# Attention and retention products on 64 rows run over all 128 rows, with zeros on the half that is not theirs

## The chip, the core and the metric

The kernel runs on one core of one Trainium2 chip. The metric is the device time of one execution in microseconds (us); before and after are compared by the median of several runs. TensorE (PE in the rows) multiplies with an array of 128 rows by 128 columns: a product first loads its stationary operand (a load of weights, PEld), then streams the moving operand through, a column at a time. The rows of the array are the contraction; an operand that stands on 64 of the 128 partitions uses 64 of them. VectorE is DVE in the rows, ScalarE is ACT, GpSimd is POOL, and SyncE, which issues the reads of the weights, is SP.

## The reference

Two layers over 256 tokens of width 2048. Each layer has a mixer (an mLSTM group, a retention group and a multi-head latent attention group side by side) and a feed-forward block. What the change touches is the scores of the attention and the retention:

```python
# attention, 8 heads: 128 columns without position, 64 with rotary position (k_r is shared by the heads)
q = concat([q[..., :128], rope(q[..., 128:])]);  k = concat([k_nope, broadcast(k_r)])
s = einsum('bqhd,bkhd->bhqk', q, k) * 192 ** -0.5
o = softmax(s) @ v

# retention, 4 heads with queries and keys of 64 columns, values of 128, in chunks of 128 tokens
scores  = einsum('bhnld,bhnsd->bhnls', qc, kc) * decay
y_intra = einsum('bhnls,bhnse->bhnle', scores, vc)
y_inter = einsum('bhnld,bhnde->bhnle', qc, r_start) * inner     # r_start: [64, 128], the state before the chunk
y       = y_intra + y_inter                                     # forward and backward are summed
```

## The kernel before

All weights are read once, in chunks of 128 partitions by 1024 columns (512 KB), in the order in which they are used. ACT rounds a chunk to its first part `whi`, DVE subtracts to get the rest `wlo`, and PE multiplies with both. These products (tile `pm`; `f` in the feed-forward) are the main stream. Four raw chunks and four split chunks may be in flight.

Everything else of the mixer is side work, written as generators whose steps are put between products of the main stream. A step yields the time to leave before its next step, and that time is counted in main-stream products issued (function `pump`). So the order of instructions on each engine is fixed when the program is built, and does not depend on how long anything takes on the chip.

The changed places, with the lines of the profile (every product goes through the helper `mm`, line 333, so the rows name the tiles):

- `mla_head(h)`, eight heads a layer. For each of the two tiles of 128 queries the scores (tile `sc`, 256 key columns) are a sum of three products: `qT` with `kT` (plain fp32, which the profile shows as two passes), `qrT` with `krh` (one pass), and `qrT` with `krl` (one pass) on partitions 0 to 63. `qrT` holds the first part of the rotated queries on partitions 0 to 63 and the second part on 64 to 127; `krh` is the first part of the rotated key on both halves, and `krl`, the second part of the key, exists on partitions 0 to 63 alone.
- `ret_task`, once a layer. It transposes queries, keys and scaled queries (tile `rt`, three groups, each copied out by ACT to `rT`), two heads to a tile: the even head on partitions 0 to 63, the odd head on 64 to 127. It also forms the states `R` (tile `rR`), laid out the same way.
- `ret_head(h)`, four heads a layer. The scores (tile `rs`) are two products of 128 columns on the 64 partitions of the head; the output (tile `ry`) is, for each of two tiles, a product on 128 partitions (`sd` with `rv`) and one on 64 (`rT` with `rR`). All of these are plain fp32, so each is two passes in the profile.

The tile `rT` takes the buffer `big2` that held the attention's `kT` before; `rsc` takes `big3` that held the attention's `v`.

Of the kernel before, what the change touches and what calls it, by code (L numbers as in the profile page):

```python
# [10 lines left out]
F32 = mybir.dt.float32  # L11
# [24 lines left out]
# columns of the constant array  # L36
# [5 lines left out]
# columns of a layer's parameter array  # L42
# [4 lines left out]
def weight_plan():  # L47
    """Blocks of weights in the order of their use; each is cut into chunks (k rows of tiles, columns)."""
    plan = []

    def nat(key, l, mat, kts, c0, w):
        per = max(1, CH // w)
        if not plan:
            kts0, kts = kts[:2], kts[2:]
            chunks = [([k], c0, w) for k in kts0]
        else:
            chunks = []
        chunks += [(kts[i:i + per], c0, w) for i in range(0, len(kts), per)]
        plan.append((key, l, mat, chunks))

    def stat(key, l, mat, kts, tiles):
        """One chunk per group of (tile, k) pairs, tile major."""
        per = CH // P
        pairs = [(t, k) for t in tiles for k in kts]
        chunks = [pairs[i:i + per] for i in range(0, len(pairs), per)]
        plan.append((key, l, mat, chunks))

    k16 = list(range(16))
    kout = [8, 9, 10, 11, 12, 13, 14, 15, 0, 1, 2, 3, 4, 5, 6, 7]
    for l in range(DEPTH):  # L70
        nat("c_q", l, "w_in", k16, 1024, 512)
        nat("c_kv", l, "w_in", k16, 1536, 336)
        nat("r_qk", l, "w_in", k16, 1872, 512)
        for h in range(0, 8, 4):
            stat(("kn", h), l, "w_kv_up", [0, 1], [h, h + 1, h + 2, h + 3])
        for b in range(2):
            nat(("v", b), l, "w_kv_up", [0, 1], 1024 + 512 * b, 512)
        for h in range(0, 8, 2):
            stat(("qn", h), l, "w_q_up", [0, 1, 2, 3], [h, h + 1])
        nat("qr", l, "w_q_up", [0, 1, 2, 3], 1024, 512)  # L80
        stat("ml_q", l, "w_in", k16, [0, 1, 2, 3])
        stat("ml_k", l, "w_in", k16, [4, 5, 6, 7])
        nat("ml_v", l, "w_in", k16, 2384, 512)
        nat("r_v", l, "w_in", k16, 2896, 512)
        nat("ml_o", l, "w_in", k16, 3408, 512)
        nat("r_g", l, "w_in", k16, 3920, 512)
        for part, kk in (("a", kout[:8]), ("b", kout[8:])):
            for b in range(2):
                nat(("out" + part, b), l, "w_out", kk, 512 * b, 512)
        for b in range(2, 4):  # L90
            nat(("out", b), l, "w_out", kout, 512 * b, 512)

        def ff1(g, i):
            f = g * 8 + 2 * i
            if g == 0 and i == 0:
                for half in range(2):
                    for t in range(2):
                        stat(("ff1", f + t, half), l, "w_ff1", k16[8 * half:8 * half + 8], [f + t])
            else:
                stat(("ff1", f), l, "w_ff1", k16, [f, f + 1])  # L100

        def ff2(g, b):
            nat(("ff2", g, b), l, "w_ff2", [g * 8 + i for i in range(8)], 512 * b, 512)

        for i in range(4):
            ff1(0, i)
        for g in range(NGRP):
            for i in range(4):
                if g + 1 < NGRP:
                    ff1(g + 1, i)  # L110
                ff2(g, i)
    return plan
# [8 lines left out]
def in_columns():  # L121
    """The columns of w_in in the order in which the blocks read them."""
    r = np.arange
    return np.concatenate([
        r(0, 1024), r(3600, 4112), r(4112, 4432), r(2048, 2064), r(2064, 2576),
        r(1024, 1536), r(2576, 3088), r(1536, 2048), r(3088, 3600)])
# [82 lines left out]
class Stream:  # L209
    """The weights, chunk after chunk: read, then split into two parts that one pass carries exactly."""  # L210
# [39 lines left out]
def encoder_kernel(ctx: ExitStack, tc: tile.TileContext, xin, posin, w, par, const, gfin, out, dump=None):  # L250
# [25 lines left out]
    rs2 = one.tile([P, 2], F32, name="rs2")  # L276
    ident = head[:, :P]
# [10 lines left out]
    nc.sync.dma_start(out=cst, in_=const)  # L288

    # the clock of the tensor engine rises with use: products of zeros until the data is there  # L290
# [14 lines left out]
    def rsqrt(dst, src, n, scale):  # L305
        """dst = 1 / sqrt(src * scale + EPS) on [P, n] by Newton's iteration, in steps."""
        nt = sp.tile([P, 3, n], F32, name="nt", tag=f"nt{n}", bufs=2 if n == 2 else 1)
        v, y, a = nt[:, 0, :], nt[:, 1, :], nt[:, 2, :]
        iv = a.bitcast(I32)
        V.tensor_scalar(v, src, scale, EPS, op0=ALU.mult, op1=ALU.add)  # L310
        V.tensor_scalar(iv, v.bitcast(I32), 1, None, op0=ALU.arith_shift_right)
        V.tensor_scalar(y.bitcast(I32), iv, -1.0, float(0x5f3759df), op0=ALU.mult, op1=ALU.add)
        for it in range(3):
            yield 1.0
            V.tensor_tensor(a, y, y, op=ALU.mult)
            V.scalar_tensor_tensor(a, a, -0.5, v, op0=ALU.mult, op1=ALU.mult)
            V.scalar_tensor_tensor(dst if it == 2 else y, a, 1.5, y, op0=ALU.add, op1=ALU.mult)

    def split(*items):
        """hi + lo = src (* g) of each item, both in the one-pass format."""  # L320
# [18 lines left out]
    class Task:  # L339
        """Steps of side work; a step yields the time to leave before the next one."""  # L340
# [46 lines left out]
    chunk_no = [0]  # L387

    def nat_steps(chunks, ps, lh, ll, base, first, last):
        """ps[t] += (lh + ll)[k].T @ weights for both tiles of tokens."""  # L390
# [22 lines left out]
    def stat(chunks, kts, rh, rl, dst):  # L413
        """dst[tile] = weights.T @ (rh + rl) for one tile of weight columns after another."""
# [26 lines left out]
    def make_xT(b, g0, l, wait):  # L441
        """Columns 512 b .. of x, transposed and times the gain; their sums of squares."""
# [28 lines left out]
    def new_xT(b, g0, l, square, wait=0.8):  # L471
        """Starts the transposes of block b; after the last, the scale of the tokens."""
# [46 lines left out]
    def rope(dst, src, t, n):  # L519
        """Rotates n heads of 64: src [P, n * 64], dst that or [P, n, 64], of tile t of the tokens."""  # L520
# [13 lines left out]
    def hflat(tl):  # L534
        return tl.rearrange("p a b -> p (a b)")

    def layer(l):
# [39 lines left out]
        def ckv_task():  # L577
# [15 lines left out]
            krl = L["krl"] = ap.tile([P, S], F32R, name="krl", tag="krl")  # L593
# [11 lines left out]
        def qr_task():  # L605
# [7 lines left out]
            # of each head the first part on 64 partitions, the second on the other 64  # L613
# [12 lines left out]
        def mla_head(h):  # L626
            qT, kT, qrT, krh, krl, v = L["qT"], L["kT"], L["qrT"], L["krh"], L["krl"], L["v"]
# [5 lines left out]
            for t in range(2):  # L633
# [4 lines left out]
                mm(o, qrT[0:64, h, tk], krl[0:64, :], False, True)  # L638
# [27 lines left out]
        def gate_task():  # L666
# [32 lines left out]
            # lf <= 0, so that the running sum is never above its last term  # L699
# [77 lines left out]
        def ml_head(h):  # L777
# [5 lines left out]
            # blocks (direction, keys, queries): F00 F01 B10 B11 B00 F11  # L783
# [57 lines left out]
        def head_out(src, stat_, gate, k0, g0):  # L841
            """Normalises the heads in src, gates them and puts them at rows k0 .. of y transposed."""
# [35 lines left out]
        def ret_task():  # L878
            rqk, v = L["rqk"], L["rv"]
            sc = ap.tile([P, 2, 512], F32, name="rsc", tag="big3")  # L880
# [6 lines left out]
            rT = ap.tile([P, 6, S], F32, name="rT", tag="big2")  # L887
            for pr in range(3):
# [6 lines left out]
                A.activation(hflat(rT[:, 2 * pr:2 * pr + 2, :]), ps, AF.Copy)  # L895
# [14 lines left out]
            L["rT"], L["rR"] = rT, R  # L910
            L["ys"] = sp.tile([P, 2, 4], F32, name="ys", tag="ys", bufs=1)

        def ret_head(h):
            v, rT, R, ys = L["rv"], L["rT"], L["rR"], L["ys"]
            yb = L["hy"][:, 1]
            hp = slice((h % 2) * 64, (h % 2) * 64 + 64)
            ps = bank("rs")
            for t in range(2):
                tk = slice(t * P, (t + 1) * P)
                mm(ps[:, tk], rT[hp, 2 + h // 2, tk], rT[hp, h // 2, tk], True, True)  # L920
# [5 lines left out]
            for t in range(2):  # L926
                o = ps[:, t * P:(t + 1) * P]
                mm(o, sd[:, t, :], v[:, t, h * P:(h + 1) * P], True, False)
                mm(o, rT[hp, 4 + h // 2, t * P:(t + 1) * P], R[hp, h // 2, 1 - t, :], False, True)
# [110 lines left out]
        hts = {}  # L1040

        def ff_evac(f, ps):
            """The square of the positive part of tile f, split."""
# [12 lines left out]
        def ff_tile(ps, chunk, first, last):  # L1056
            """ps = [hi.T x + lo.T x's first part | hi.T x's second part]."""
# [72 lines left out]
    def last_block(chunks, lh, ll):  # L1130
        """The last columns, one tile of tokens after the other, each followed by its norm."""
# [83 lines left out]
```

## Time and profile before

| | |
|---|---|
| time, median of 3 runs | 2184.02 us (2183.72 to 2184.79) |
| the profiled execution, first to last instruction | 2183.1 us |
| PE busy | 2164.9 us, 99% |
| load of weights (PEld) | 1840.8 us, 84% |
| DVE busy | 1354.7 us, 62% |
| ACT busy | 1044.0 us, 48% |
| POOL busy | 0.2 us, four instructions |
| chain of work that ended last, share of PE | 95% |

The profiled execution's span is within 1 us of the median of the runs, so terms that are read from the trace can be taken from the median. PE is busy for nearly all of the span, but "busy" runs from the start of a product to its modelled end, and products overlap; a pause between two products that is shorter than this overlap does not show as idle time of PE. It shows in the load of weights, or in the distance between the ends of products.

### The profile page before, as it was taken

What the parts mean: (1) busy time and instruction counts of PE and PEld (TensorE: products, weight loads), DVE (VectorE), ACT (ScalarE), POOL (GpSimd) and SP (SyncE); (2) the same over time, 40 slices, a digit from 0 to 9 for tenths busy, and PEclk for the clock granted to TensorE, in tenths of its full rate; (3) what the DMA queues carried; (4) which work ended last, traced back from release to release, by engine and by line L of the source; (5) the groups of instructions that cost most, each with busy time, mean ns of one, the idle gap of its engine ahead of it and who ended that gap; (6) DMA issues with size and microseconds to landing.
All of it is one profiled execution on the core that took longest, in us unless ns stands there. A gap on an engine that the chain in (4) does not pass through costs nothing.

```text
span 2183.1 us, 29259 instructions
## 1 busy us (share of the span) xinstructions
PE 2164.9 (99%) x11280; PEld 1840.8 (84%) x11280; DVE 1354.7 (62%) x2019; ACT 1044.0 (48%) x1530; POOL 0.2 (0%) x4
## 2 busy tenths in 40 slices
PE   8999999999999999999999999999999999999998
PEld 7898888888888888888888978888888888888887
DVE  5667565666565656566666575756656565656655
ACT  5645655444444444444556455545444444444444
POOL 0000000000000000000000000000000000000000
PEclk9999999999999999999999999999999999999999
DMA  7544555566555556565565354555555555656554
GB/s 217 186 135 134 165 163 186 172 193 197 188 194 191 194 186 200 181 201 180 189 181 173 118 165 133 167 190 183 196 189 194 188 197 184 202 178 207 175 204 162
DMA packets 111356, 395.20 MB, mean 181 GB/s; under 512 B 12904, under 2 KB 14056, under 8 KB 111088
## 3 DMA queue, kind: packets, MB, share of 16 engines
q1 hardware_dynamic: 109072, 389.90, 54.7%
q10 hardware_dynamic: 2144, 3.43, 0.5%
q8 instruction: 88, 1.44, 0.3%
q14 instruction: 52, 0.43, 0.1%
HBM read 391.17 MB, written 2.12 MB: 180 GB/s over the span
## 4 chain that ended last, share of the span: by engine, by line
PE 95%; DVE 2%; ACT 1%; DMA 1%; issue 1%; ACTq 0%; SPq 0%; DVEq 0%
PE pm L333 57%; PE f L333 33%; PE sc L333 1%; DMA wraw<-in_w_dram 1%; DVE wlo L238 1%; PE o L333 1%; ACT whi L237 1%; PE ry L333 1%; PE num L333 0%; PE xt L330 0%; PE pt L330 0%; PE st L333 0%; ACT junk L303 0%; PE rs L333 0%; DVE mqk L765 0%
## 5 line engine op out<-in xcount | busy, mean ns | idle before, releaser
L238 DVE TENSOR_TENSOR wlo<-wraw,whi 128x1024 fp32r<-128x1024 f32 (+2 forms) x737 | 875.1, 1217 | 275.9 <-ACT whi L237 274.3
L237 ACT ACTIVATE whi<-wraw 128x1024 fp32r<-128x1024 f32 (+2 forms) x737 | 749.9, 1048 | 333.0 <-PE pm L333 286.6
L333 PE MATMUL f<-xT,whi 128*128 128x512 f32 x2048 | 712.0, 392 | 0.0
L333 PE MATMUL f<-xT,wlo 128*128 128x256 f32 x2048 | 552.1, 280 | 0.0
L333 PEld LDWEIGHTS f<-xT,whi 128*128 128x128 f32 x2048 | 379.4, 188 | 77.0
L333 PE MATMUL pm<-wlo,hhi 128*128 128x512 f32 (+1 forms) x1040 | 401.6, 386 | 0.6 <-DVE wlo L238 0.6
L333 PE MATMUL pm<-whi,hhi 128*128 128x512 f32 (+1 forms) x1040 | 402.1, 387 | 0.0
L333 PE MATMUL pm<-whi,hlo 128*128 128x512 f32 (+1 forms) x1040 | 401.2, 386 | 0.0
L333 PEld LDWEIGHTS f<-xT,wlo 128*128 128x128 f32 x2048 | 385.0, 188 | 11.3 <-DVE wlo L238 0.8
L333 PE MATMUL pm<-whi,xT 128*128 128x512 f32 (+1 forms) x896 | 291.3, 394 | 2.4 <-ACT whi L237 1.4
L333 PEld LDWEIGHTS pm<-wlo,hhi 128*128 128x128 f32 x1040 | 195.4, 188 | 40.2 <-DVE wlo L238 1.0
L333 PEld LDWEIGHTS pm<-whi,hlo 128*128 128x128 f32 x1040 | 195.4, 188 | 39.7
L1051 ACT ACTIVATE fr<-f 128x256 f32<-128x256 f32 x128 | 49.1, 384 | 374.3 <-PE f L333 374.3
L333 PEld LDWEIGHTS pm<-whi,hhi 128*128 128x128 f32 x1040 | 195.4, 188 | 37.2
L333 PEld LDWEIGHTS pm<-whi,xT 128*128 128x128 f32 x896 | 167.2, 189 | 37.5 <-ACT whi L237 1.6
L1052 DVE TENSOR_TENSOR fr<-f,fr 128x256 f32<-128x256 f32 x128 | 54.3, 424 | 218.0 <-ACT fr L1051 218.0
L1024 DVE SCALAR_TENSOR_TENSOR xx<-pm,rs,xx 128x512 f32<-128x512 f32 x126 | 90.1, 751 | 144.3 <-PE pm L333 144.3
L333 PE MATMUL pm<-wlo,xT 128*128 128x512 f32 (+1 forms) x448 | 173.5, 387 | 2.4 <-DVE wlo L238 2.3
L322 ACT ACTIVATE hhi<-fq 128x256 fp32r<-128x256 f32 x128 | 53.5, 418 | 126.8 <-DVE fq L1053 126.8
L333 PE MATMUL pm<-whi,yhi 128*128 128x512 f32 x256 | 101.5, 397 | 0.0
L333 PEld LDWEIGHTS pm<-wlo,xT 128*128 128x128 f32 x448 | 84.9, 189 | 19.6 <-DVE wlo L238 4.9
L333 PE MATMUL pm<-whi,ylo 128*128 128x512 f32 x256 | 99.8, 390 | 0.0
(235 smaller groups left out, 1614.7 us busy)
## 6 DMA issues: line engine op xcount, KB each, us to landing
wraw<-in_w_dram SPq DMA_DIRECT2D x723, 512.0 KB, 4.2
wraw<-in_w_dram SPq DMA_DIRECT2D x10, 504.0 KB, 6.7
wt<-mx_rows ACTq DMA_DIRECT2D x8, 256.0 KB, 3.7
out_dram<-xx SPq DMA_DIRECT2D x8, 256.0 KB, 3.3
xx<-in_x_dram SPq DMA_DIRECT2D x3, 512.0 KB, 8.1
gf<-in_gfin_dram ACTq DMA_DIRECT2D x1, 1024.0 KB, 6.1
xx<-in_x_dram SPq DMA_DIRECT2D x2, 256.0 KB, 3.8
wraw<-in_w_dram SPq DMA_DIRECT2D x2, 256.0 KB, 4.5
```

What stands on the lines that cost most here:

```text
L237: self.nc.scalar.activation(hi[:, :f], raw[:, :f], AF.Copy)
L238: self.nc.vector.tensor_tensor(lo[:, :f], raw[:, :f], hi[:, :f].bitcast(F32), op=ALU.subtract)
L322: A.activation(hi, src, AF.Copy, **({"scale": g[0]} if g else {}))
L333: T.matmul(ps, lhsT=lhsT, rhs=rhs, start=start, stop=stop)
L1024: V.scalar_tensor_tensor(x[t][:, xs], ps[t], scale[:, t:t + 1], x[t][:, xs], op0=ALU.mult, op1=ALU.add)
L1051: A.activation(r, ps[:, S:], AF.Copy)
L1052: V.tensor_tensor(r, ps[:, :S], r, op=ALU.add)
```

## The change

All products of these places now use 128 partitions. `krl` becomes a tile that lives for the whole kernel; POOL fills it with zeros once at the start, and each layer writes partitions 0 to 63 as before. In the retention, the keys stay two heads to a tile (now in the third part of `rsc`), while queries and scaled queries go to a new tile `rq` with a full 128-partition slot for each head, which POOL fills with zeros once a layer and into which ACT writes the 64 partitions of the head. The sums are the same, since the half that is not the head's is multiplied by zero.

```diff
+    krl = one.tile([P, S], F32R, name="krl")
...
+    nc.gpsimd.memset(krl.bitcast(F32), 0.0)
...
-            krl = L["krl"] = ap.tile([P, S], F32R, name="krl", tag="krl")
...
-                mm(o, qrT[0:64, h, tk], krl[0:64, :], False, True)
+                mm(o, qrT[:, h, tk], krl, False, True)
...
-            sc = ap.tile([P, 2, 512], F32, name="rsc", tag="big3")
+            big = ap.tile([P, 3, 512], F32, name="rsc", tag="big3")
+            sc, rT = big[:, 0:2, :], big[:, 2, :].rearrange("p (a b) -> p a b", a=2)
+
+            qz = ap.tile([P, 2, 4, S], F32, name="rq", tag="big2")
+            nc.gpsimd.memset(qz.rearrange("p a b c -> p (a b c)"), 0.0)
...
-            rT = ap.tile([P, 6, S], F32, name="rT", tag="big2")
...
-                A.activation(hflat(rT[:, 2 * pr:2 * pr + 2, :]), ps, AF.Copy)
+                if pr == 1:
+                    A.activation(hflat(rT), ps, AF.Copy)
+                else:
+                    for j in range(2):
+                        hp = slice(j * 64, j * 64 + 64)
+                        A.activation(qz[hp, pr // 2, j:4:2, :],
+                                     ps[hp, :].rearrange("p (a b) -> p a b", a=2), AF.Copy)
...
-            hp = slice((h % 2) * 64, (h % 2) * 64 + 64)
...
-                mm(ps[:, tk], rT[hp, 2 + h // 2, tk], rT[hp, h // 2, tk], True, True)
+                mm(ps[:, tk], rT[:, h // 2, tk], rq[:, 0, h, tk], True, True)
...
-                mm(o, rT[hp, 4 + h // 2, t * P:(t + 1) * P], R[hp, h // 2, 1 - t, :], False, True)
+                mm(o, rq[:, 1, h, t * P:(t + 1) * P], R[:, h // 2, 1 - t, :], False, True)
```

On ACT the copies of the retention's transposes stand between the splits of the weights (`whi`). Before, in layer 0:

```order
L237 ACTIVATE whi_2375<-wraw_2259 128x1024
L895 ACTIVATE rT<-rt 128x512 x2
L237 ACTIVATE whi_2414<-wraw_2290 128x1024
L895 ACTIVATE rT<-rt 128x512
L907 ACTIVATE rR<-rst 64x256 x2
L237 ACTIVATE whi_2460<-wraw_2322 128x1024
```

And after, in the same place:

```order
L237 ACTIVATE whi_2378<-wraw_2260 128x1024
L905 ACTIVATE rq<-rt 64x2x256 x2
L901 ACTIVATE rsc<-rt 128x512
L237 ACTIVATE whi_2417<-wraw_2291 128x1024
L905 ACTIVATE rq<-rt 64x2x256 x2
L918 ACTIVATE rR<-rst 64x256 x2
L237 ACTIVATE whi_2464<-wraw_2323 128x1024
```

Two copies of 128 partitions by 512 have become four of 64 partitions by 512; the splits around them have not moved.

On PE the products stand in the same order as before. This is the output of retention head 0 and the scores of head 1 behind it, before:

```order
L333 MATMUL ry<-rv,sd 128x128
L333 MATMUL ry<-rR,rT 128x128
L333 MATMUL ry<-rv,sd 128x128
L333 MATMUL ry<-rR,rT 128x128
L333 MATMUL rs<-rT 128x128 x2
L333 MATMUL pm<-whi_2460,xT 128x512
```

And after:

```order
L336 MATMUL ry<-rv,sd 128x128
L336 MATMUL ry<-rR,rq 128x128
L336 MATMUL ry<-rv,sd 128x128
L336 MATMUL ry<-rR,rq 128x128
L336 MATMUL rs<-rq,rsc 128x128 x2
L336 MATMUL pm<-whi_2464,xT 128x512
```

Only the operands differ; a size in these rows is that of the output, which has 128 partitions either way.

## Rows read from the trace of the kernel before

**Rows 1.** The page: the span, and busy time, share and instructions by engine.
```profile
span 2183.1 us, 29259 instructions
PE 2164.9 (99%) x11280; PEld 1840.8 (84%) x11280; DVE 1354.7 (62%) x2019; ACT 1044.0 (48%) x1530; POOL 0.2 (0%) x4
```

**Rows 2.** The waits of the load of weights: us in total, times, longest.
```profile
PEld sc L333 <- issue: 7.4, 32, 0.2
```

**Rows 3.** Timeline of PE, attention head 0: start us, length us, products, xcount.
```profile
130.39 0.47 PE L333 MATMUL sc<-krh,qrT 128*128 128x256 f32 x1
130.79 0.38 PE L333 MATMUL sc<-krl,qrT 64*128 64x256 f32 x1
131.10 0.70 PE L333 MATMUL sc<-kT,qT 128*128 128x256 f32 x2
131.45 0.47 PE L333 MATMUL sc<-krh,qrT 128*128 128x256 f32 x1
```

**Rows 4.** The chain in order of time, attention: start us, us, work, passes.
```profile
127.49 2.82 PE pm L333 x24
130.31 1.92 PE sc L333 x8
132.22 3.01 PE pm L333 x24
...
185.29 1.92 PE sc L333 x8
```

**Rows 5.** The chain in order of time, retention of layer 0.
```profile
250.44 0.89 PE rst L333 x8
251.33 2.81 PE pm L333 x12
254.14 0.86 PE st L333 x4
255.00 0.64 PE rs L333 x4
255.64 2.99 PE pm L333 x12
258.63 1.36 PE ry L333 x7
259.99 0.01 PE rs L333
260.00 0.11 PE ry L333
260.10 0.23 PE rs L333 x3
260.33 1.59 PE pm L333 x6
...
264.66 1.47 PE ry L333 x8
```

**Rows 6.** Groups by tile (krl, rT), whole run: ns min/median/max, first and last start.
```profile
L333 PE MATMUL sc<-krl,qrT x32: 380/381/384, 130.8 to 1268.0; 64*128 64x256 f32 x32
L333 PE MATMUL rs<-rT x32: 272/272/373, 254.9 to 1358.2; 64*128 64x128 f32 x32
```

**Rows 7.** The chain and PE's timeline after the last attention head.
```profile
191.50 2.79 PE pm L333 x12
...
214.39 0.50 PE L333 MATMUL pm<-wlo,xT 128*128 128x512 f32 x1 [0.36 <-DVE wlo L238]
```

**Rows 8.** Timeline of ACT, the copies of the retention's transposes.
```profile
242.42 0.60 ACT L895 ACTIVATE rT<-rt 128x512 f32<-128x512 f32 x1 [2.97 <-PE rt L330]
244.92 0.60 ACT L895 ACTIVATE rT<-rt 128x512 f32<-128x512 f32 x1 [1.90 <-PE rt L330]
```

**Rows 9.** Groups of memsets: busy us, mean ns of one, idle us before.
```profile
L1204 POOL MEMSET const-float32-1.0<- 128x1 f32 x1 | 0.1, 99 | 0.0
...
L292 DVE MEMSET warm<- 128x256 uint32 x1 | 0.3, 272 | 0.9 <-PEq L1204 0.9
```

More of the change, by code (lines that the diff above doesn't have):

```diff
@@ L626, in mla_head @@
         def mla_head(h):
-            qT, kT, qrT, krh, krl, v = L["qT"], L["kT"], L["qrT"], L["krh"], L["krl"], L["v"]
+            qT, kT, qrT, krh, v = L["qT"], L["kT"], L["qrT"], L["krh"], L["v"]
             if h == 0:
@@ L909, in ret_task @@
                 yield 1.2
-            L["rT"], L["rR"] = rT, R
+            L["rT"], L["rq"], L["rR"] = rT, qz, R
             L["ys"] = sp.tile([P, 2, 4], F32, name="ys", tag="ys", bufs=1)
         def ret_head(h):
-            v, rT, R, ys = L["rv"], L["rT"], L["rR"], L["ys"]
+            v, rT, rq, R, ys = L["rv"], L["rT"], L["rq"], L["rR"], L["ys"]
             yb = L["hy"][:, 1]
-            hp = slice((h % 2) * 64, (h % 2) * 64 + 64)
             ps = bank("rs")
```

## The prediction

> **What bounds the kernel now.** I read the page first: PE is busy for 2164.9 of 2183.1 us [rows 1], so a microsecond matters here only if it is one in which PE produces nothing, and those must be sought inside its busy time. The list of waits gives a first sign. The load of weights for the scores `sc` stood idle 32 times, 7.4 us in all (0.23 each), with no releaser [rows 2]: no semaphore held it up. Thirty-two is also the number of products with `krl` [rows 6]. So I went to PE's timeline there, and then to the chain of work, which adds up runs of products.
>
> In the timeline I compare ends (start plus length), not starts, since a product starts while the one ahead is still draining. Between two attention products on 128 rows [rows 3]: `krh` ends at 130.86; the 64-row `krl` at 131.17, 0.31 later; the two passes of the next `kT` at 131.80, 0.63 later; the next `krh` at 131.92, 0.12 later. The steady pace is known from undisturbed runs of products in the chain: 2.82 us for 24 one-pass products of 256 columns, so 0.1175 each [rows 4]; 0.86 for four fp32 passes of 256, so 0.215; 0.89 for eight fp32 passes of 128, so 0.111; 2.81 for twelve of 512, so 0.234 [rows 5]. `krl` therefore lost 0.31 - 0.12 = 0.19, and the `kT` behind it 0.63 - 0.43 = 0.20. The step from `kT` (fp32) to `krh` (one pass) lost nothing, so it is not the change of number format that costs. What costs is going from 128 rows to 64, and again going back.
>
> The chain says the same with less rounding. The eight passes of one head's scores take 1.92; at the steady pace they would take 4 x 0.215 + 4 x 0.1175 = 1.33. That is 0.59 for three changes, and the fourth is seen behind them: 24 `pm` take 3.01 instead of 2.82 [rows 4]. A head pays 0.78 for four changes, 0.195 each. In the retention four passes of `rs` take 0.64 instead of 0.44, the twelve `pm` behind them 2.99 instead of 2.81, and `ry` (eight passes, three changes inside) 1.47 instead of 0.89, so 0.18 to 0.20 each [rows 5]. I take 0.19.
>
> **The sum, part by part.**
>
> *Attention.* Two layers, eight heads, two tiles: 32 stays on 64 rows [rows 6], each with a change in and one out. 64 x 0.195 = 12.5 us gone. The product itself stays: `krl` on 128 rows costs what `krh` costs, since the pace follows the columns (0.111 for 128 fp32 columns on 128 rows in `rst`, and the same 0.11 for such a pass of `rs` on 64, four of which take 0.64 less one change).
>
> *Retention.* A head has one stay for `rs` and two for `ry`, 12 a layer. In one place the `rs` of head 1 stands directly behind the last `ry` of head 0, with no 128-row product between them, so there are 11 stays and 22 changes a layer. 44 x 0.19 = 8.4 us gone.
>
> *What is lost in that one place.* Here the two heads use opposite halves, and the trace shows them at the same time: after seven passes of `ry`, the last `ry` and four passes of `rs` take 0.01 + 0.11 + 0.23 = 0.35 instead of 5 x 0.111 = 0.555 [rows 5]. On 128 rows they go one behind the other: 0.20 a layer, 0.4 in all, given back. The Trainium skill has this as a rule that speaks against the change ("TensorE: Matmul & The Clock Gate", Part 3: Packing small matmuls): products on different row groups run concurrently, and the gain of small contractions is that concurrency. By that rule alone one would expect a loss here. The rows bear it out for this one place a layer; everywhere else the neighbour of a 64-row product uses the full array or the same half.
>
> *ACT.* In each layer two copies of 128 by 512 become four of 64 by 512. I price all at the 0.60 of the old ones [rows 8], so 1.2 us more a layer, 2.4 in all. ACT stood idle for 2.97 and 1.90 us ahead of the first two old copies, waiting for PE's transposes, and the new pair replaces the first, so I take nothing and keep 2.4 as the bound.
>
> *POOL.* Three memsets: 256 columns once, at the start, and 2048 columns once a layer. The trace has none of this size. Below, the rate of DVE's memset (256 words in 0.27 us) gives 2.2 us; above, if each column cost what POOL's memset of one column costs, 0.1 us x 2048 = 203 us [rows 9]. The small one has most of its 0.1 us from being an instruction at all, so I take about 2 us. It may begin once the last head's scores have read `kT`, at 187.2 [rows 4], and is first needed by ACT's copy at 242.4 [rows 8]: 55 us of cover, in which POOL has nothing else. A memset of 2 us is hidden. No row shows POOL at work beside DVE. If DVE stood still for its length and PE had to wait all of it, it would cost 2 x 2.2 = 4.4 us; if they don't touch, nothing. I take nothing, since DVE is busy for 62% [rows 1] and such a wait would first use up its idle time. The Trainium skill ("SBUF — State Buffer", Who interferes with whom) has the two engines share a port pair as an exclusive lock, but lets a GpSimd instruction that only writes pass beside most DVE instructions; no run so far shows it.
>
> *Where the stream could catch up.* A faster PE asks for weights sooner. Behind the last attention head the chain leaves PE after the products that end at 194.29, runs through ACT and DVE (the convolution and gating of the mLSTM's keys, and splits of weights among them), and comes back to PE at 214.39, where PE waited 0.36 us for `wlo` [rows 7]. No 64-row product lies in this stretch, and the ACT and DVE work in it starts from PE's own products, so it moves forward with them. I take the 0.36 as unchanged. In the retention the chain is PE alone.
>
> Sum: 12.5 + 8.4 - 0.4 = 20.5 us, all on the path. The profiled execution has a span of 2183.1 [rows 1], 0.9 under the median of the runs, 2184.0, from which I subtract: **2163.5 us**.
>
> **The rivals.**
>
> *Part of the gain runs into ACT and DVE (7%).* If the stretch from 194 to 214 did not start sooner, because a split of weights or a read in front of it is already late, the whole gain of the attention would be waited out there: 8.4 - 0.4 = 8.0 us left, 2176. A partial loss lies between, 2168 to 2176. For it: PE already waits there. Against it: the chain enters the stretch from PE, and over the heads before it the chain is made of PE's products, with no wait for a split among them [rows 4].
>
> *The pause is not that of the rows (3%).* If the 0.19 came with the place (the order of accumulation, an operand, the wait ahead of it) and not with 64 against 128 rows, the products would keep it, and ACT's 2.4 could come on top: 2184 to 2186. Against it: passes of 64 rows behind 64 rows flow without a pause, in three different products the pause appears at both borders, and the `pm` that pays at the far border has nothing else in common with them.
>
> *Slower: POOL's memset is late (2%).* ACT waits for it at the copy into `rq`, and behind that copy on ACT's queue stand the splits of the weights, so PE would starve. It decides from about 55 us of cover + up to 8 us of splits that are ready (three chunks ahead, each worth the 2.81 us of twelve `pm`) + 10 us gained a layer, so from a memset of 73 us, 36 ns a column. At POOL's one-column price, 203 us, each layer would lose 203 - 63 = 140: 2163.5 + 280 = 2443. DVE's rate is 1.06 ns a column, thirty times below the point of decision, hence the low chance.
>
> **How the numbers follow.** The forecast has 88%, the rivals 7, 3 and 2. Low end: 0.20 for every change gives 108 x 0.20 - 0.4 = 21.2, so 2162.8, and the runs scatter by about a microsecond: 2161.7. High end: ACT's 2.4 on the path, or half of POOL's 4.4, gives 2166; a little of the first rival brings 2167.5. A measurement of this kernel can tell about 0.2%, 4.4 us, from no change. The forecast and the first rival lie below 2179.6: faster 0.95; the second rival is within the bound: 0.03; the third beyond it: slower 0.02.
>
> **What the new profile would show.** Right: no product of 64 rows; a head's `sc` 1.33 in the chain and the 24 `pm` behind it 2.82; `rs` 0.44 for four passes, `ry` 0.89 for eight, and `ry` with `rs` at the one double place at 0.111 a pass; no waits of `sc` loads on "issue"; PE busy near 2145 in a span near 2162.6; PE's wait at the `wlo` behind the last head still about 0.4; two memsets on POOL of some 2 us that nobody waits for. Wrong: a pause of 0.19 left at `krl` on 128 rows (second rival); `pm` waiting longer for `wlo` behind the last head, or new waits on `whi` around the copies into `rq` (first and third).

## The result, and the profile after

The changed kernel takes 2164.23 us (median of 4 runs, 2163.05 to 2164.72) against 2183.99 before (4 runs, 2183.72 to 2184.79): a ratio of 0.9909 with a 95% interval of 0.9895 to 0.9923, or 19.8 us less. The forecast was 20.5 us less, 2163.5. The profiled execution has a span of 2162.9 us, 20.2 less than that of before.

The page of the changed kernel, in the lines that answer to [rows 1]; POOL has three more instructions, its memsets:

```profile
span 2162.9 us, 29276 instructions
PE 2144.4 (99%) x11280; PEld 1837.5 (85%) x11280; DVE 1355.2 (63%) x2019; ACT 1047.5 (48%) x1534; POOL 4.1 (0%) x7
```

PE has as many products as before and is busy for 20.5 us less. ACT and POOL are busy for 3.5 and 3.9 us more, with the added copies and memsets. So PE lost no work; what it lost are pauses inside its busy time, as the chain shows.

The chain of the changed kernel, attention head 0 and 1 with the main stream around them (start us, us, work, passes):

```profile
127.78 2.82 PE pm L336 x24
130.60 1.33 PE sc L336 x8
131.93 2.82 PE pm L336 x24
134.75 1.35 PE sc L336 x8
136.09 2.85 PE pm L336 x24
...
139.38 1.44 PE pm L336 x12
```

Against [rows 4] the eight passes of a head went from 1.92 to 1.33 (1.35 in head 1), and the 24 products behind them from 3.01 to 2.82 (2.85 behind head 1): what the steady pace gave in the prediction, with no pause of 0.19 left at either border. The last row shows twelve products at 0.120 instead of 0.1175, of which more below.

The chain in the retention of layer 0:

```profile
249.26 0.44 PE rs L336 x4
249.70 2.80 PE pm L336 x12
252.50 0.89 PE ry L336 x8
253.39 0.45 PE rs L336 x4
253.84 1.41 PE pm L336 x6
...
257.98 0.89 PE ry L336 x8
```

Against [rows 5], `rs` went from 0.64 to 0.44, the products behind it from 2.99 to 2.80, and `ry` from 1.47 to 0.89. The double place shows the one loss: the last pass of `ry` and four of `rs` took 0.35 before, partly at the same time; now the four of `rs` alone take 0.45, one behind the other. Twelve passes there still went from 1.36 + 0.35 = 1.71 to 1.34, since three changes fell away.

The waits of the load of weights no longer have a row for `sc`, where [rows 2] had 7.4 us. The groups of tile `krl` (ns min/median/max) show the product at the duration of any one-pass product of 256 columns, 0.28 us; it was 0.38 [rows 6]:

```profile
L336 PE MATMUL sc<-krl,qrT x32: 277/280/285, 131.0 to 1252.5; 128*128 128x256 f32 x32
```

The additions, from ACT's timeline, the groups of POOL, and PE's timeline behind the last attention head:

```profile
236.74 1.20 ACT L905 ACTIVATE rq<-rt 64x512 f32<-64x512 f32 x2 [3.03 <-PE rt L333]
239.18 0.60 ACT L901 ACTIVATE rsc<-rt 128x512 f32<-128x512 f32 x1 [1.24 <-PE rt L333]
```

```profile
L886 POOL MEMSET rq<- 128x2048 f32 x2 | 3.6, 1812 | 1249.8 <-PE sc L336 1249.8
L291 POOL MEMSET krl<- 128x256 f32 x1 | 0.3, 312 | 0.3 <-POOLq L1214 0.3
```

```profile
208.65 0.50 PE L336 MATMUL pm<-wlo,xT 128*128 128x512 f32 x1 [0.35 <-DVE wlo L238]
```

A copy of half a tile costs the 0.60 of a whole one (two in 1.20), and ACT still waits for PE before each [rows 8]. A memset of 2048 columns takes 1.81 us. PE's wait for `wlo` behind the last head is 0.35, as it was 0.36 [rows 7].

### The profile page after: what moved, and what is told of

It reads as the page before. It is cut to its first block, busy times and chain, and to the rows that moved or that the text cites. A ratio compares the mean times of both kernels' runs of the same rounds, so it can differ in the third digit from the quotient of the medians.

```text
span 2162.9 us, 29276 instructions
## 1 busy us (share of the span) xinstructions
PE 2144.4 (99%) x11280; PEld 1837.5 (85%) x11280; DVE 1355.2 (63%) x2019; ACT 1047.5 (48%) x1534; POOL 4.1 (0%) x7
## 3 DMA queue, kind: packets, MB, share of 16 engines
q8 instruction: 88, 1.44, 0.3%
## 4 chain that ended last, share of the span: by engine, by line
PE 94%; DVE 2%; ACT 1%; DMA 1%; issue 1%; ACTq 0%; SPq 0%; DVEq 0%
PE pm L336 57%; PE f L336 33%; DMA wraw<-in_w_dram 1%; PE sc L336 1%; DVE wlo L238 1%; PE o L336 1%; ACT whi L237 1%; PE num L336 0%; PE xt L333 0%; PE ry L336 0%; PE pt L333 0%; PE st L336 0%; ACT junk L306 0%; DVE mqk L767 0%; DVE mqk L757 0%
```

## The experiments

Each is compared with the kernel before on the same chip. "The changed kernel" below is the one of this result.

**The attention alone.** The kernel before, with `krl` as a zeroed tile and only this product changed:

```diff
-                mm(o, qrT[0:64, h, tk], krl[0:64, :], False, True)
+                mm(o, qrT[:, h, tk], krl, False, True)
```

> Only the attention's product with krl runs over 128 rows; the retention is as before. Theory (each change between 64 and 128 rows costs PE 0.195 us, and nothing else matters): 64 changes gone, 2184.0 - 12.5 = 2171.5 us, and a head's scores take 1.33 us in the chain, while the retention's rs still take 0.64 and ry 1.47. Rival (part of the gain runs into ACT and DVE behind the last head): the wait for wlo behind the last head grows by as much as the time lies above 2171.5.

Measured: 2170.78 against 2183.23 us, ratio 0.9944 (0.9932 to 0.9957), 12.4 us less. Behind the last head PE waits 0.4 us for `wlo`, as before, so nothing of the gain is waited out there and the rival, a gain lost in ACT and DVE, falls. The chain has both prices side by side, a head of the attention without and the retention with its changes:

```profile
128.78 1.33 PE sc L335 x8
130.11 2.82 PE pm L335 x24
...
247.44 0.64 PE rs L335 x4
248.08 2.99 PE pm L335 x12
...
257.10 1.47 PE ry L335 x8
```

**The retention alone.** The changed kernel, with this product back on its half:

```diff
-                mm(o, qrT[:, h, tk], krl, False, True)
+                mm(o, qrT[0:64, h, tk], krl[0:64, :], False, True)
```

> Only the retention's products run over 128 rows; krl is a full tile but its product uses partitions 0 to 63 as before. Theory: 44 changes gone, 0.4 us of overlap lost, 2184.0 - 8.0 = 2176.0 us; a head's scores stay at 1.92. With attention_alone the two gains must add up to that of the whole change, 19.8 us. Rival (ACT's more numerous copies or POOL's memset cost something): the gain is smaller than 8.0 by up to 2.4 to 4.4.

Measured: 2175.20 against 2183.23 us, ratio 0.9965 (0.9952 to 0.9977), 8.0 us less. The two parts make 20.5 us together; the whole change made 19.8. They add up to within what the runs scatter, about a microsecond and a half.

**The additions alone.** As the retention alone, and the retention's products go back to their halves too, in the new tiles:

```diff
+            hp = slice((h % 2) * 64, (h % 2) * 64 + 64)
...
-                mm(ps[:, tk], rT[:, h // 2, tk], rq[:, 0, h, tk], True, True)
+                mm(ps[:, tk], rT[hp, h // 2, tk], rq[hp, 0, h, tk], True, True)
...
-                mm(o, rq[:, 1, h, t * P:(t + 1) * P], R[:, h // 2, 1 - t, :], False, True)
+                mm(o, rq[hp, 1, h, t * P:(t + 1) * P], R[hp, h // 2, 1 - t, :], False, True)
```

> Everything that the change adds is there (the zeroed tiles, POOL's memsets, four copies of half a tile a layer), but all products use only their own 64 partitions of these tiles. Theory: the pause belongs to the rows of the product, the additions are hidden: 2184.0 us, within 0.5. Rival (the pause came from the old tiles, buffers or waits): about 2164. Rival (additions on the path): up to 2186.4 by ACT, 2188.4 by POOL beside DVE.

Measured: 2183.22 against 2183.23 us, ratio 1.0000 (0.9991 to 1.0009). The memsets, the tiles, their buffers and the extra copies neither cost nor gain anything that can be measured, which here means more than 2 us. The second rival of the prediction falls, since with the same tiles and the same order the pauses are back in the chain:

```profile
129.32 1.92 PE sc L336 x8
131.23 3.02 PE pm L336 x24
...
254.02 0.64 PE rs L336 x4
```

**One stay a head.** The kernel before; the second tile's `krl` product opens its sum instead of closing it, and so stands directly behind the first tile's. As many products, half as many changes:

```diff
+                if t == 1:
+                    mm(o, qrT[0:64, h, tk], krl[0:64, :], True, False)
-                mm(o, qT[:, h, tk], kT[:, h, :], True, False)
-                mm(o, qrT[:, h, tk], krh, False, False)
-                mm(o, qrT[0:64, h, tk], krl[0:64, :], False, True)
+                mm(o, qT[:, h, tk], kT[:, h, :], t == 0, False)
+                mm(o, qrT[:, h, tk], krh, False, t == 1)
+                if t == 0:
+                    mm(o, qrT[0:64, h, tk], krl[0:64, :], False, True)
```

> The kernel before, but in each attention head the krl product of the second tile of queries is put first in its sum, directly behind the krl product of the first tile. As many 64-row products as before, half as many changes. Theory (price per change): 32 changes gone, 2184.0 - 6.2 = 2177.8 us, a head's eight passes take 1.33 + 2 x 0.195 = 1.72 in the chain with nothing on the pm behind them. Rival (price per 64-row product): 2184.

Measured: 2177.10 against 2183.23 us, ratio 0.9973 (0.9963 to 0.9983), 6.1 us less. The chain:

```profile
129.25 1.73 PE sc L333 x8
130.98 2.82 PE pm L333 x24
```

1.73 = 1.33 + 2 x 0.20, and nothing on the products behind. The price is per change, not per product of 64 rows.

**An extra product, of 64 rows, 128 rows, 32 rows, and 64 columns.** The changed kernel, with one product more behind each of the 128 tiles of the first feed-forward product. Its result is read by nobody.

```diff
+            z = bank("z")
+            mm(z[:, :S], krl[0:64, :P], krl[0:64, :], True, True)
```

The others have `krl[:, :P]` with `krl`, `krl[0:32, :P]` with `krl[0:32, :]`, and `krl[:, :64]` with `krl` into `z[0:64, :S]`.

> The changed kernel, with one product of 64 rows by 256 columns (krl with itself, into a bank that nobody reads) behind each of the 128 tiles of the first feed-forward product, where all neighbours use 128 rows. Theory (0.195 for each change, in and out, wherever it stands): 2164.2 + 128 x (0.1175 + 0.39) = 2229 us. Rival (the pause needs something of the attention and retention, such as an open sum or fp32 neighbours): 2164.2 + 15 = 2179.

> The same with all 128 rows of krl. Theory: only the columns count, 2164.2 + 128 x 0.1175 = 2179 us. The difference to extra_64_rows, divided by 256, is the price of a change by itself: 0.195 expected. Rival (an extra bank or product of itself costs the pause): as extra_64_rows.

> The same with 32 rows. Theory (a change is a change, whatever the number of rows): 2229 us, as with 64. Rival (the price follows the rows that fall idle): 2179 + 50 x 96/64 = 2254.

> The same product on all 128 rows, but with a stationary operand of 64 columns, so that the output has 64 partitions. Theory (it is the rows that must be the same as the neighbours'): 2179 us, as with 128 rows. Rival (any other shape of the array than 128 by 128 pays): 2229, as with 64 rows.

| extra product | us | ratio to before |
|---|---|---|
| 64 rows | 2228.80 | 1.0201 (1.0186 to 1.0217) |
| 128 rows | 2181.25 | 0.9985 (0.9976 to 0.9994) |
| 32 rows | 2229.12 | 1.0203 (1.0188 to 1.0218) |
| 128 rows, 64 columns | 2178.85 | 0.9974 (0.9964 to 0.9984) |

Against the full product, 64 rows cost (2228.80 - 2181.25) / 256 = 0.186 us for each change; against the one of 64 columns 0.195. The full product stands 2.3 us above its forecast and 2.4 above the one of 64 columns. That is not its price in the chain, which is 0.12 for both; in the profiled executions PE waits 5.5 us for `wlo` with 128 columns and 3.9 with 64, and the rest is not accounted for. The chain shows one such product with 64 rows, then one with 128:

```profile
501.20 0.31 PE z L336
501.51 5.74 PE f L336 x32
```

```profile
517.11 0.12 PE z L336
517.22 5.56 PE f L336 x32
```

It takes 0.31 instead of 0.12 with the change in, and the 32 `f` behind it 5.74 instead of 5.56 with the change back: 0.19 and 0.18. So the pause needs nothing of the attention or retention. It is the same for 32 rows as for 64, and a stationary operand of fewer columns doesn't have it. The load of weights of `z` stood idle 126 times on 64 rows, 31.1 us in all, with no releaser, like that of `krl` in [rows 2]; on 128 rows it has no such wait. What the array does in this time no run shows.

**Two heads side by side.** The attention as changed, the retention on 64 rows in the tiles of before, but two heads at a time, in banks of their own (the step of the generator now does two heads and yields 3.2). The core of it:

```diff
+            for t in range(2):
+                tk = slice(t * P, (t + 1) * P)
+                for j, h in enumerate(hs):
+                    mm(ps[j][:, tk], rT[hps[j], 2 + h // 2, tk], rT[hps[j], h // 2, tk], True, True)
...
+            intra(0)
+            for t in range(2):
+                tk = slice(t * P, (t + 1) * P)
+                for j, h in enumerate(hs):
+                    mm(ps[j][:, tk], rT[hps[j], 4 + h // 2, tk], R[hps[j], h // 2, 1 - t, :], t == 1, t == 0)
+            intra(1)
```

`intra(t)` is the product of `sd` with `rv` of tile `t` for both heads; it stands ahead of the 64-row products for the first tile of tokens and behind them for the second.

> Attention as changed; the retention on 64 rows again, but two heads at a time, so that products on the lower and the upper half alternate, in different banks, and one stay serves both heads. Theory (products on opposite halves run at the same time, and a stay costs two changes): for two heads rs takes 4 x 0.111 + 0.39 = 0.83 instead of 8 x 0.111 = 0.89, ry saves the same 0.06, so 0.5 us under the changed kernel, 2163.7 us: a draw. Rival (they run one behind the other): 8 stays x 0.39 more than the changed kernel, 2167.3.

Measured: 2165.57 against 2183.63 us, ratio 0.9917 (0.9902 to 0.9932): no different from the whole change's 0.9909. The chain, and the waits of PE:

```profile
247.36 0.65 PE rs L335 x8
...
253.06 1.52 PE ry L335 x14
```

```profile
PE num L335 <- DVE wt L799: 2.0, 2, 1.0
```

Eight passes `rs` of two heads take 0.65 with the change in, that is 4 x 0.111 + 0.20. The fourteen of `ry`, eight of them on 64 rows, take 1.52: 10 x 0.111 + 0.39 is 1.50, while 14 x 0.111 + 0.39 would be 1.94. So products on opposite halves do run at the same time, in both places. With the change out `rs` makes 0.84, against 0.89 for zeros. The time is 1.9 us above the 2163.7 expected, and a wait that is new can hold it: 1.0 us a layer of the mLSTM's products `num` for DVE. The chain into this wait runs through ACT's and DVE's work on the output and the decay of two heads at a time; which of it delays DVE was not tested.

**POOL's memset 40 times.**

```diff
-            nc.gpsimd.memset(qz.rearrange("p a b c -> p (a b c)"), 0.0)
+            for _ in range(40):
+                nc.gpsimd.memset(qz.rearrange("p a b c -> p (a b c)"), 0.0)
```

> The changed kernel, with POOL's memset of rq done 40 times over, 72.5 us a layer at the 1.81 us that one took. Theory (the memset is hidden by the time between the last head's scores and ACT's first copy, 55 us, and then by three split chunks, 8 us): ACT waits some 17 us, PE loses about 9 us a layer: 2182 us, with a wait of PE for whi or wlo near the first copy. Rival (POOL's writes hold up DVE): the wait for wlo already grows in the 72 us in which POOL works, and the time is above 2190.

Measured: 2202.65 against 2183.63 us, ratio 1.0087 (1.0070 to 1.0104): 38 us above the changed kernel, where 18 were expected, so the rival was right that there was a second loss. PE's waits (us in total, times, longest):

```profile
PE rt L333 <- ACT rq L906: 18.7, 2, 9.3
PE pm L336 <- DVE wlo L238: 10.8, 11, 2.6
PE pt L333 <- DVE pr L653: 4.5, 4, 1.6
```

The first row is the expected wait, 9.3 us a layer, though PE meets it at the third group of the retention's transposes, whose bank ACT's late copies have to empty first, not at a split of weights. Behind it PE ran slowly. The wait and the two stretches behind it, in each row the busy time of PE, PEld, DVE, ACT and POOL, then the granted clock, then the share and rate of the DMA:

```profile
248.00:257.00 9.00, 0.12 (x1) 0.00 (x0) 0.00 (x0) 0.76 (x2) 7.96 (x5) 0.78 0.00 0
257.00:263.00 6.00, 5.53 (x19) 4.94 (x20) 3.77 (x14) 3.13 (x6) 0.00 (x0) 0.50 0.25 79
263.00:270.00 7.00, 7.00 (x37) 5.93 (x36) 2.31 (x4) 6.88 (x17) 0.00 (x0) 0.98 0.35 121
```

After 9.3 us without a product the clock stood at half (0.50), the 1.2 GHz level, until about 263. The second and third rows of the waits are new, too: neither stands in that size in the changed kernel, and the waits for `pr` lie far ahead of ACT's copy, at the last attention head (189 to 191 us in layer 0), while POOL works.

**POOL's memset 12 times**, to separate the two losses (the same edit with `range(12)`).

> The changed kernel with POOL's memset of rq done 12 times over: about 22 us a layer, over long before ACT's first copy into rq, so that ACT can't wait for it. Theory (memset_40_times lost in two ways: 9.3 us a layer by ACT's wait and a slow clock behind it, and some 7 us a layer because VectorE's TENSOR_SCALAR stands still while a memset of POOL runs): TENSOR_SCALAR takes up to 1.9 us in that stretch, the transposes pt wait for pr behind the last heads as with 40 memsets, and 4 to 7 us a layer are lost: 2172 to 2178. Rival (all was lost by ACT's wait): 2164.

Measured: 2175.30 against 2184.51 us, ratio 0.9957 (0.9944 to 0.9971): some 10 to 11 us above the changed kernel, 5 a layer, without any wait of ACT for POOL. So the rival, that all was lost by ACT's wait, falls. PE's waits have the same row for `pr` as with 40 memsets:

```profile
PE pt L333 <- DVE pr L653: 4.5, 4, 1.6
```

Between 180 and 220 us PE waits 2.2 us for `pr` and 2.2 for `wlo`; in the changed kernel it is 0.4, for `wlo` alone. VectorE's groups between 181 and 204 us (busy us, mean ns of one), first here, with one instruction from the timeline (start us, length us), then in the changed kernel with its single memset:

```profile
L238 DVE TENSOR_TENSOR wlo<-wraw,whi 128x1024 fp32r<-128x1024 f32 x5 | 6.1, 1221 | 3.2 <-ACT whi L237 3.2
L756 DVE TENSOR_SCALAR mqk<-mt,head 128x256 f32<-128x256 f32 x4 | 5.3, 1316 | 0.0
L653 DVE TENSOR_SCALAR pr<-pr,sm 128x256 f32<-128x256 f32 x2 | 3.3, 1690 | 0.0
L757 DVE SCALAR_TENSOR_TENSOR mqk<-mt,head,mqk 128x255 f32<-128x255 f32 x4 | 1.9, 484 | 0.1
```

```profile
190.57 1.97 DVE L756 TENSOR_SCALAR mqk<-mt,head 128x256 f32<-128x256 f32 x1
```

```profile
L238 DVE TENSOR_TENSOR wlo<-wraw,whi 128x1024 fp32r<-128x1024 f32 x7 | 8.5, 1219 | 3.2 <-ACT whi L237 3.2
...
L757 DVE SCALAR_TENSOR_TENSOR mqk<-mt,head,mqk 128x255 f32<-128x255 f32 x6 | 2.9, 484 | 0.2
L756 DVE TENSOR_SCALAR mqk<-mt,head 128x256 f32<-128x256 f32 x6 | 2.4, 400 | 0.0
...
L653 DVE TENSOR_SCALAR pr<-pr,sm 128x256 f32<-128x256 f32 x2 | 0.6, 352 | 0.0
```

A TENSOR_SCALAR of 256 columns, which takes 0.35 us alone, takes up to 1.97: it stands for 1.62 us, less than the 1.8 of one memset. The SCALAR_TENSOR_TENSOR between them keeps its 0.48 to the nanosecond, and the split of weights (a TENSOR_TENSOR) its 1.22.

The Trainium skill ("SBUF — State Buffer", Who interferes with whom) has this: DVE and GpSimd share a port pair as an exclusive lock, `tensor_scalar` can take it in its two-port modes, and an instruction with two inputs in SBUF passes beside a GpSimd instruction that only writes. Which instructions stood and which passed agrees with it (1.97 against 0.48 and 1.22 us); the ports and the modes themselves are not in the trace.

In the changed kernel the single memset touches two TENSOR_SCALAR a layer (in layer 0 `mx` takes 0.61 us instead of 0.17, `mqk` 0.67 instead of 0.35). That is some 0.8 us of VectorE's time, and in the run of the additions alone it cost nothing that can be measured.

## Why the prediction was right

- *What bounds the kernel, and the price of a change.* Right, in the mechanism too. Reading the ends of products gave 0.195 us for each change between 64 and 128 rows, invisible in PE's busy share. The extra products, far from attention and retention, give 0.186 to 0.195 for the same thing by itself, and halving the changes at equal work gave half of the attention's gain (6.1 of 12.4 us).
- *Attention, 12.5 us forecast.* 12.4 by the runs. By the traces 12.0: from the first `sc` to the first product of the feed-forward it is 386.0 - 130.1 = 255.9 us before, and 378.5 - 128.6 = 249.9 with the attention alone. The half microsecond between shows in the chain: in some places between the heads the main stream runs at 2.85 instead of 2.82 or 1.44 instead of 1.41, and most heads take 1.34 or 1.35 instead of 1.33. Why is open.
- *Retention, 8.4 less 0.4 for the lost overlap.* 8.0 by the runs, and by the traces 2 x (255.9 - (380.7 - 128.9)) = 8.2. The overlap that was given up is real: at the double place the last pass of `ry` and four of `rs` went from 0.35 to 0.11 + 0.45, the 0.2 a layer forecast. But where two heads' products stand between full ones, the overlap only makes up for the two changes: 0.84 against 0.89 us.
- *ACT and POOL at nothing.* Right in sum (ratio 1.0000 with the additions alone, to within 2 us). ACT's copies cost the 1.2 us a layer forecast, under cover. POOL's memset took 1.81 us, forecast about 2. Of the two reasons given for POOL one held. A memset does pass beside most of VectorE's instructions, but not beside TENSOR_SCALAR, an exception that the prediction's "most" left open. Its other reason, that a wait would first use up VectorE's idle time, held for the single memset (0.8 us a layer, for which no wait of PE appears), but not for twelve in a row, though VectorE's busy share over the whole span is 63% in both.
- *The stretch behind the last head moves with PE.* Right: PE's wait there is 0.35, and the attention's gain came through whole.
- *The slower rival* was not the case, but its point of decision was misplaced: it counted 73 us, where gain and loss would be even, from ACT's wait alone. Twelve memsets, 22 us, already cost 5 us a layer by way of VectorE, and at 40 memsets, 73 us, the kernel was 19 us slower than before.
- The remaining difference to the measured time, 0.7 us, is no larger than the scatter of the runs (2163.05 to 2164.72). In the profiled execution the first `sc` starts at 130.4 us, 0.3 later than before; with the attention, the retention and the additions alone it starts at 128.6, 128.9 and 129.2. So the stretch in front of it varies by more than the difference.

## What to carry to other kernels

In a stream of products on the full array, a product on fewer rows paid here for the change in and the change back: 0.39 us, more than the 0.12 of the product itself (one pass of 256 columns). If the place of such a product is fixed, fill the unused rows with zeros: here a pass cost by its columns, and the zeros were free as long as writing them was hidden. Where products on fewer rows can stand next to each other, count stays and not products; pairs on opposite halves then came out even with zeros. Such pauses don't show in TensorE's busy share (99% before and after): compare the ends of successive products with the pace of an undisturbed run.

## What the runs showed of the hardware that was not expected

- A change between 128 rows and 64 costs 0.19 us each way, and the change to 32 rows costs the same (2229.12 and 2228.80 us), while a stationary operand of 64 columns costs nothing over one of 128 (2178.85 and 2181.25 us).
- A memset of POOL (1.81 us) stops VectorE's TENSOR_SCALAR for nearly its own length (1.97 us for one that takes 0.35), and leaves SCALAR_TENSOR_TENSOR (0.48) and TENSOR_TENSOR (1.22) alone.
- Behind a wait of 9.3 us TensorE's granted clock was 0.50 for about 6 us of work.
